# Two interleaved mixers on one TensorE queue: its order taken from the source, value products one key block later, PSUM banks rearranged

## The chip, the cores and the metric

One NeuronCore of a Trainium2 chip runs the whole kernel. The metric is the device time of one execution in microseconds (us). An engine runs its own queue of instructions in order: PE is TensorE (matmuls), DVE VectorE, ACT ScalarE, POOL GpSimd, SP the queue that issues most transfers.

## What is computed

The reference is an encoder block of one layer (2048 tokens, width 1024). Its first half mixes tokens: one projection feeds a bidirectional softmax attention (8 heads of 64, two key heads) and a bidirectional RWKV-7 recurrence (8 heads of 64); their outputs are joined, projected and added. Its second half is an expert-choice mixture of 16 SwiGLU experts. The part that the change touches:

```python
s = jnp.einsum('bqhgd,bkhd->bhgqk', qi, k, preferred_element_type=jnp.float32) * scale
p = jax.nn.softmax(s, axis=-1).astype(v.dtype)
o = jnp.einsum('bhgqk,bkhd->bqhgd', p, v)
...
sa = jnp.einsum('bhvk,bhk->bhv', S, -kk_t)
S = (S * w_t[:, :, None, :] + sa[..., None] * (kk_t * a_t)[:, :, None, :]
     + v_t[..., None] * k_t[:, :, None, :])
y_t = jnp.einsum('bhvk,bhk->bhv', S, r_t)
```

## The kernel before, in words

The program has four parts: `phase1` (projections and preparation, to about 720 us), `mixers` (attention and recurrence together, to about 2375 us), `out_proj` and `moe`. Only `mixers` changes. It draws on two Python generators in turn, `rwkv` and `attention`, which record instructions. A scheduler then sets the order on each engine from priorities and its own times, so PE's order is not the source's.

**Attention** has 16 blocks of 512 queries (for two heads). A block walks over 16 key blocks `kb`. For each: four matmuls make the scores (tile `st`, one buffer of two banks, L707 and L708), ACT takes the exponential into a tile `pt` (L709, four buffers, `PTB`), DVE and POOL add `pt` to the row sums `acc` (L712). After four key blocks a group of eight matmuls multiplies the four `pt` with the values (tile `o_ps`, L694), at high priority and before the scores of the next key block; it begins with the `pt` that came last. At a block's end `sum_ps` (L674), a reciprocal of 512 columns (L676) and a product finish it. Meanwhile `att_max` finds the maxima for the next block: 32 pairs of matmuls into `s_ps` (L648, L649, two banks) and 32 DVE reductions (L650). Block 7 is the last of the first key head; there the next block's maxima wait for new keys.

**Recurrence**: 16 groups `n` (four pairs of heads, two directions, two halves of the sequence), each of four quarters `k`, each quarter of four turns `j` (one `yield` a turn). A quarter `i` does: `rq_step` (L1030, the state of the quarter before, ACT scales it at L1035) in every turn; `rq_l` (tile `l_ps`, L1013, into `lc` by ACT L1015 and DVE L1016) in turns 0 and 1; `a1_rows` (four transposes, L852) in turn 2; `rq_av` (two transposes of `al` into `av_ps`, L980) and `rq_wu` (L1001) in turn 3. Two jobs are put off (`self.tiled`) until the next value group, and `flush` records them behind it: `a1_products` (L865, into the banks of `st`; two DVE products with a mask take it out, L870) and the products into `av_ps` (L988; ACT copies all of it into `r4`, L990). `rq_wu` multiplies `r4` with the group's inverse `tt`.

Three banks serve this: `pa` (transposes, merge), `pb` (`av_ps`, `wu_ps`, both halves of `l_ps`), `pc` (steps). One tile holds a bank until the last reader is done.

The inverse `tt` of group `n+1` is made during group `n`: `rw_solve` (30 elimination steps of two small operations, L901 and L903, for nine groups all on DVE, for seven all on POOL; three steps a turn in quarters 0 to 2), a round of transfers through DRAM, and `rw_merge` in quarter 3: transfers into `bdn`, `bdr`, `tt`; eight matmuls `z_ps` (L940, ACT copy L941), eight `x_ps` (L946), four ACT copies into `tt` (L949).

Of the kernel before, what the change touches and what calls it, by code (L numbers as in the profile page):

```python
# [12 lines left out]
ALU = mybir.AluOpType  # L13
# [570 lines left out]
PTB = 4  # L584
# [5 lines left out]
class Attention(Encoder):  # L590
# [32 lines left out]
    def att_max(self, j, qc, keys, res):  # L623
# [5 lines left out]
        for h in range(2):  # L629
            qd = self.a_q.tile([P, 512], F32, tag="q_raw", name="q_raw")  # L630
# [31 lines left out]
        mt = self.a_q.tile([16, P], F32, tag="mt", name="mt")  # L662
# [7 lines left out]
    def att_finish(self, j, qc, av, acc):  # L670
# [9 lines left out]
    def att_out(self, keys, v, q):  # L680
        nc = self.nc
        khh, kl1 = keys
        qs, q2 = q
        av = self.o_ps.tile([P, 512], F32, tag="o", name="o_ps")
        acc = self.a_l.tile([P, 2, 512], F32, tag="acc", name="acc")
        pts = {}

        def group(k0):
            with self.tc.high_priority():

                for kb in (k0 + 3, k0, k0 + 1, k0 + 2):
                    pt = pts.pop(kb)
                    for h in range(2):
                        last = nc.tensor.matmul(av[64 * h : 64 * h + 64, :], v[:, kb, :], pt[:, h, :], start=(kb == 3), stop=(kb == 14), tile_position=(0, 64 * h))  # L694
                with self.tc.issue_after(last.ins):
                    self.behind = self.flush() or last.ins

        for kb in range(16):
            ks = slice(kb * P, (kb + 1) * P)

            if kb % 4 == 0 and kb:
                group(kb - 4)
            pt = self.a_p.tile([P, 2, 512], F32, tag="pt", name="pt", bufs=PTB)
            pts[kb] = pt
            s = self.o_ps.tile([P, 2, 512], F32, tag="st", name="st_ps", bufs=1)
            for h in range(2):
                nc.tensor.matmul(s[:, h, :], khh[:, ks], qs[h], start=True, stop=False)  # L707
                nc.tensor.matmul(s[:, h, :], kl1[:, ks], q2[h], start=False, stop=True)  # L708
            nc.scalar.activation(out=pt, in_=s, func=AF.Exp, scale=0.125)  # L709
            if kb:  # L710
                for h, eng in enumerate((nc.gpsimd if kb % 8 == 3 else nc.vector, nc.gpsimd)):
                    eng.tensor_tensor(out=acc[:, h, :], in0=(first if kb == 1 else acc)[:, h, :], in1=pt[:, h, :], op=ALU.add)  # L712
            else:
                first = pt
            if kb >= 6 and self.block in MOD_BLOCKS:
                next(self.rest, None)
            yield
        group(12)
        self.att_done = av, acc

    def attention(self):

# [6 lines left out]
        while more:  # L729
# [3 lines left out]
            if n % 3 == 0:  # L733
                yield
        v = self.att_values(0)
        done = None
        for n, (j, qc) in enumerate(blocks):
            if n == 7:
                nxt, nq, late = None, [], True
            else:  # L740
                nq, late = [], False
                nxt = self.att_max(*blocks[n + 1], keys, nq) if n + 1 < 16 else iter(())
            if done:
                self.att_finish(*done)
            self.block = n
            for _ in self.att_out(keys, v, cur):
                if not late:
                    for _ in range(3):
                        next(nxt, None)
                yield  # L750
            done = (j, qc) + self.att_done
            if late:
                keys = self.att_keys(1)
                for i, _ in enumerate(self.att_max(*blocks[n + 1], keys, nq)):
                    if i % 3 == 2:
                        yield
# [5 lines left out]
        self.att_finish(*done)  # L762
# [8 lines left out]
SOLVE_DVE = (0, 2, 4, 5, 7, 8, 11, 12, 14)  # L771


class Rwkv(Attention):
# [110 lines left out]
    def rw_solve(self, n, g):  # L885
# [3 lines left out]
        eng = nc.vector if n in SOLVE_DVE else nc.gpsimd  # L889
# [82 lines left out]
    def rq_av(self, Q):  # L972
# [5 lines left out]
        p3 = self.bank("pb").tile([P, 2, 4, 64], F32, tag="p", name="av_ps")  # L978
        for i in range(2):
            nc.tensor.transpose(p3[:, i, 0:4:3, :], Q["al"][:, i, :], self.ident)  # L980
        lv = l56.rearrange("p c (x k) -> p c x k", k=64)

        def products():
            for r in range(2):
                for h in range(2):
                    for par in range(2):
                        c = 2 * r + par
                        last = nc.tensor.matmul(p3[64 * par : 64 * par + 64, r, 1 + h, :], r56[64:128, c, 192 * h : 192 * h + 64],  # L988
# [670 lines left out]
```

## Time and profile before

| | us |
|---|---|
| median of 3 runs (3774.88 to 3779.12) | 3778.05 |
| the profiled execution | 3788.53 |
| its span in the trace | 3786.8 |
| PE busy in the span | 3415.4 (90%) |
| DVE, ACT, POOL busy | 2529.6, 1737.5, 1513.7 |

Busy time of PE is the time in which at least one matmul is in flight; a slow clock makes it longer. PEclk is the clock granted to TensorE as a share of full speed.

### The profile page before, as it was taken

The numbers are of one execution on the slowest core, as the hardware profiler recorded it, in microseconds if no ns is written. First come the engines' busy times: TensorE is split into PE (matmuls) and PEld (weight loads), VectorE is DVE, ScalarE is ACT, GpSimd is POOL, SyncE is SP. The second block draws the span as 40 slices with busy tenths as digits, with TensorE's granted clock in tenths as the row PEclk, the third lists the DMA queues.
The fourth block names the chain that finished last, engine by engine and source line by source line (L and its number), as shares of the span: only waits on it lengthen the run. The fifth ranks groups of instructions, "written<-read, shape, count | busy, mean of one in ns | idle before, by whom it ended". The sixth has DMA issues, their size and how long they took to land. (4 is left out here: it accounts for less than half of the span.)

```text
span 3786.8 us, 61015 instructions
## 1 busy us (share of the span) xinstructions
PE 3415.4 (90%) x23196; PEld 2811.8 (74%) x23196; DVE 2529.6 (67%) x4289; ACT 1737.5 (46%) x3050; POOL 1513.7 (40%) x1484
## 2 busy tenths in 40 slices
PE   6998899779988888898889998994999999999998
PEld 5887888656666566576666665773899999999997
DVE  5788788875858957665886866446565665655653
ACT  4445444415554455445555565222344444444443
POOL 3444345516363363456347275332332322322321
PEclk8999999779998999889999998997999999999999
DMA  5335333443323433433333322443566766766764
GB/s 180 106 126 174 105 117 137 145 129 74 86 66 89 105 90 73 101 81 87 86 83 92 79 69 80 155 151 117 165 214 212 215 215 205 223 201 217 222 200 129
DMA packets 531866, 511.16 MB, mean 135 GB/s; under 512 B 213624, under 2 KB 450530, under 8 KB 526452
## 3 DMA queue, kind: packets, MB, share of 16 engines
q1 hardware_dynamic: 521252, 472.34, 40.6%
q0 software_dynamic: 10000, 34.91, 4.0%
q8 instruction: 183, 3.00, 0.3%
q14 instruction: 111, 0.91, 0.1%
q10 hardware_dynamic: 320, 0.00, 0.0%
HBM read 392.70 MB, written 109.20 MB: 133 GB/s over the span
## 5 line engine op out<-in xcount | busy, mean ns | idle before, releaser
L1496 DVE TENSOR_TENSOR w_lo<-w_raw,w_hi 128x2048 fp32r<-128x2048 f32 x189 | 432.8, 2295 | 385.9 <-ACT w_hi L1493 385.3
L1560 PE MATMUL gu<-hh,w_lo 128*128 128x256 f32 x2048 | 573.3, 280 | 0.0
L1560 PE MATMUL gu<-hl,w_hi 128*128 128x256 f32 x2048 | 572.4, 280 | 0.0
L1560 PE MATMUL gu<-hh,w_hi 128*128 128x256 f32 x2048 | 572.4, 280 | 0.0
L712 POOL TENSOR_TENSOR acc<-acc,pt 128x512 f32<-128x512 f32 x256 | 346.6, 1359 | 507.2 <-ACT pt L709 471.0
L1493 ACT CAST w_hi<-w_raw 128x2048 fp32r<-128x2048 f32 x192 | 366.9, 1912 | 320.0 <-PE down L1583 133.3
L650 DVE TENSOR_REDUCE mx<-s_ps 128x1 f32<-128x512 f32 x512 | 337.6, 681 | 131.1 <-PE s_ps L649 128.6
L247 PE MATMUL proj_ps<-hh,w_hi 128*128 128x258 f32 (+1 forms) x1280 | 375.4, 294 | 32.9 <-DVE s_k L265 23.9
L1560 PEld LDWEIGHTS gu<-hh,w_lo 128*128 128x128 f32 x2048 | 387.8, 189 | 0.0
L1560 PEld LDWEIGHTS gu<-hh,w_hi 128*128 128x128 f32 x2048 | 385.5, 188 | 1.3
L1560 PEld LDWEIGHTS gu<-hl,w_hi 128*128 128x128 f32 x2048 | 385.5, 188 | 1.4
L247 PE MATMUL proj_ps<-hl,w_hi 128*128 128x258 f32 (+1 forms) x1280 | 373.1, 292 | 6.4 <-DVE hl L149 5.9
L247 PE MATMUL proj_ps<-hh,w_lo 128*128 128x258 f32 (+1 forms) x1280 | 371.6, 290 | 0.0
L709 ACT ACTIVATE pt<-st_ps 128x1024 f32<-128x1024 f32 x256 | 262.1, 1024 | 209.1 <-PE st_ps L708 168.5
L149 POOL TENSOR_TENSOR dl<-hid,dh 128x256 fp32r<-128x256 f32 x128 | 135.1, 1055 | 448.1 <-ACT dh L148 447.8
L694 PE MATMUL o_ps<-pt,av 128*64 128x512 f32 x1024 | 269.9, 675 | 27.5 <-ACT pt L709 27.2
L247 PEld LDWEIGHTS proj_ps<-hh,w_hi 128*128 128x128 f32 x1280 | 250.9, 196 | 41.8 <-issue 23.0
L648 PE MATMUL s_ps<-khh,qhl 128*128 128x512 f32 x512 | 239.7, 469 | 33.5 <-DVE mx L650 28.4
L707 PE MATMUL st_ps<-qhl,khh 128*128 128x512 f32 x512 | 231.8, 453 | 38.0 <-DVE r L870 31.5
L247 PEld LDWEIGHTS proj_ps<-hl,w_hi 128*128 128x128 f32 x1280 | 251.5, 197 | 10.6 <-DVE hl L149 6.6
L247 PEld LDWEIGHTS proj_ps<-hh,w_lo 128*128 128x128 f32 x1280 | 250.7, 196 | 2.1 <-issue 1.1
L712 DVE TENSOR_TENSOR acc<-acc,pt 128x512 f32<-128x512 f32 x192 | 189.0, 984 | 63.4 <-ACT pt L709 60.4
(418 smaller groups left out, 7979.2 us busy)
## 6 DMA issues: line engine op xcount, KB each, us to landing
w_raw<-in_w_gate_dram SPq DMA_DIRECT2D x64, 1024.0 KB
w_raw<-in_w_up_e_dram SPq DMA_DIRECT2D x64, 1024.0 KB
w_raw<-in_w_down_dram SPq DMA_DIRECT2D x64, 1024.0 KB
d_x<-X SPq DMA_DIRECT2D x32, 1024.0 KB
xin<-d_x SPq DMA_DIRECT2D x64, 512.0 KB
w_raw<-in_w_in_dram SPq DMA_DIRECT2D x80, 256.0 KB
mod_w<-in_w_ada_dram SPq DMA_DIRECT2D x64, 256.0 KB
mod_w<-in_w_ada_dram SPq DMA_DIRECT2D x8, 1024.0 KB
```

The lines of the kernel that those rows point to most:

```text
L149: (eng or nc.gpsimd).tensor_tensor(out=lo, in0=src, in1=hi.bitcast(F32), op=ALU.subtract)
L247: nc.tensor.matmul(acc[:, :n], a[:, kt, :], b[:, kt, lo : lo + n], start=(kt == 0 and m == 0), stop=(kt == KT - 1 and m == 2))
L648: nc.tensor.matmul(s, qs[h][:, ts], khh[:, ks], start=True, stop=False)
L650: nc.vector.tensor_reduce(out=mx[:, 4 * h + qt, kc : kc + 1], in_=s, axis=AX.X, op=ALU.max)
L694: last = nc.tensor.matmul(av[64 * h : 64 * h + 64, :], v[:, kb, :], pt[:, h, :], start=(kb == 3), stop=(kb == 14), tile_position=(0, 64 * h))
L707: nc.tensor.matmul(s[:, h, :], khh[:, ks], qs[h], start=True, stop=False)
L709: nc.scalar.activation(out=pt, in_=s, func=AF.Exp, scale=0.125)
L712: eng.tensor_tensor(out=acc[:, h, :], in0=(first if kb == 1 else acc)[:, h, :], in1=pt[:, h, :], op=ALU.add)
L1493: nc.scalar.copy(out=hi, in_=raw)
L1496: eng.tensor_tensor(out=lo, in0=raw, in1=hi.bitcast(F32), op=ALU.subtract)
L1560: nc.tensor.matmul(acc[:, m, :], a[:, kt, i * P : (i + 1) * P], b[:, kt, :], start=(kt == 0 and n == 0), stop=(kt == KT - 1 and n == 2))
```

## The change

PE's order inside `mixers` is now the source's (`manual_schedule`); the other engines are still ordered by the scheduler. The two generators are drawn on in small parts: `yield False` ends a part, `yield True` a turn, and the two alternate part by part until both have ended the turn. A value group is recorded after the scores of the next key block (for a block's last group after the first scores of the next block), with the sums' matmuls behind it; `pt` gets a fifth buffer, two small tiles lose their second. The transposes of `al` go to bank `pa` with their own ACT copy, the second half of `l_ps` to `pa` too. Every solve has its first 12 steps on DVE and the other 18 on POOL. In quarter 3 the merge's transfers are issued in turn 0, `z_ps` in turn 2, `x_ps` in turn 3. The reciprocal is four of 128 columns. A gap in `out_proj`'s memory map grows by 1536 bytes.

```diff
@@ constants @@
-PTB = 4
+PTB = 5
...
-SOLVE_DVE = (0, 2, 4, 5, 7, 8, 11, 12, 14)
+SOLVE_DVE = 12
@@ att_finish: the sums' matmuls leave it, the reciprocal in four pieces @@
-        sm = self.a_ps.tile([P, 512], F32, tag="s", name="sum_ps", bufs=SB)
-        for h in range(2):
-            nc.tensor.matmul(sm[64 * h : 64 * h + 64, :], self.ones[:, 0:64], acc[:, h, :], start=True, stop=True, tile_position=(0, 64 * h))
         rec = self.a_l.tile([P, 512], F32, tag="rec", name="rec")
-        nc.vector.reciprocal(out=rec, in_=sm)
+        for c in range(0, 512, P):
+            nc.vector.reciprocal(out=rec[:, c : c + P], in_=sm[:, c : c + P])
@@ att_out becomes att_values_of, att_scores, att_sums @@
-            with self.tc.high_priority():
-
-                for kb in (k0 + 3, k0, k0 + 1, k0 + 2):
...
+    def att_values_of(self, B, k0):
...
+        with self.tc.issue_after(B["st"]):
+            for kb in range(k0, k0 + 4):
+                pt = B["pts"].pop(kb)
+                for h in range(2):
+                    last = nc.tensor.matmul(av[64 * h : 64 * h + 64, :], v[:, kb, :], pt[:, h, :], start=(kb == 0), stop=(kb == 15), tile_position=(0, 64 * h))
+            if k0 == 12:
+                sm = self.a_ps.tile([P, 512], F32, tag="s", name="sum_ps", bufs=SB)
...
+        with self.tc.issue_after(last.ins):
+            self.behind = self.flush() or last.ins
+        if k0 == 12:
+            self.att_finish(*B["id"], av, sm)
@@ attention: one key block a turn, in small steps @@
+            for kb in range(16):
+                for i in range(4 if kb % 4 == 2 else 3):
+                    if kb % 4 or kb == i:
+                        next(nxt, None)
+                    yield False
+                self.att_scores(B, kb)
+                if kb % 4 == 0 and (kb or last):
+                    if kb == 0:
+                        last["st"] = B["st"]
+                    self.att_values_of(B if kb else last, kb - 4 if kb else 12)
+                if kb:
+                    self.att_sums(B, kb)
...
+                yield True
@@ rw_solve @@
-        eng = nc.vector if n in SOLVE_DVE else nc.gpsimd
...
         for i in range(1, 31):
...
+            eng = nc.vector if i <= SOLVE_DVE else nc.gpsimd
@@ rq_av @@
-        p3 = self.bank("pb").tile([P, 2, 4, 64], F32, tag="p", name="av_ps")
+        pt = self.bank("pa").tile([P, 2, 2, 64], F32, tag="p", name="al_ps")
         for i in range(2):
-            nc.tensor.transpose(p3[:, i, 0:4:3, :], Q["al"][:, i, :], self.ident)
+            nc.tensor.transpose(pt[:, i], Q["al"][:, i, :], self.ident)
+        r4v = r4.rearrange("p r (x k) -> p r x k", k=64)
+        nc.scalar.copy(out=r4v[:, :, 0:4:3, :], in_=pt)
...
         def products():
+            p3 = self.bank("pb").tile([P, 2, 2, 64], F32, tag="p", name="av_ps")
...
-            nc.scalar.copy(out=r4, in_=p3.rearrange("p r x k -> p r (x k)"))
+            nc.scalar.copy(out=r4v[:, :, 1:3, :], in_=p3)
@@ rq_l @@
-        p5 = self.bank("pb").tile([P, 4, P], F32, tag="p", name="l_ps")
+        p5 = self.bank("pa" if h else "pb").tile([P, 4, P], F32, tag="p", name="l_ps")
@@ rwkv: extra(j), and each turn j in three parts @@
-                if k == j == 0:
-                    pass
-                elif k < 3:
-                    run(solve, 3)
-                else:
+                if k < 3:
+                    run(solve, 3 if k + j else 0)
+                elif j == 0:
                     run(solve)
+                    run(merge, 1)
+                elif j == 2:
                     run(merge, 2)
                 run(fin, 1)
...
             step(0)
+            yield False
             self.rq_l(Qs[i], 0)
...
+            yield False
             extra(0)
-            yield
+            yield True
@@ mixers @@
-        streams = [self.rwkv(), self.attention()]
-        n = 0
-        while streams:
-            n += 1
-            for g in list(streams):
-                if len(streams) == 2 and g is streams[1] and n % 4 == 0 and n <= 12:
-                    continue
-                if next(g, "end") == "end":
-                    streams.remove(g)
+        streams = [self.attention(), self.rwkv()]
+        with self.tc.manual_schedule(engines={mybir.EngineType.PE}):
+            n = 0
+            while streams:
+                n += 1
+
+                turn = [g for g in streams if len(streams) == 1 or g is streams[1] or n % 4 or n > 12]
+                while turn:
+                    for g in list(turn):
+                        done = next(g, "end")
+                        if done:
+                            turn.remove(g)
+                        if done == "end":
+                            streams.remove(g)
```

On PE, at the end of a quarter, the value group with what hangs on it stands like this before (`o_ps` values, `av_ps` and `p` the two put-off jobs, `s_ps_` with a number the recurrence's step, `s_ps` the maxima, `st_ps` scores):

```order
L694 MATMUL o_ps<-pt,av 64x512 x8
L988 MATMUL av_ps<-l_0_8385,r_10367 64x64 x8
L865 MATMUL p_11756<-xin 128x128 x8
L1030 MATMUL s_ps_11790<-sr_8373,lc 128x64 x2
L648 MATMUL s_ps<-khh,qhl 128x512
L649 MATMUL s_ps<-kl_8312,qa 128x512
L648 MATMUL s_ps<-khh,qhl 128x512
L649 MATMUL s_ps<-kl_8312,qa 128x512
L1001 MATMUL wu_ps<-r_11519,tt_8368 128x128 x4
L1030 MATMUL s_ps_11790<-sr_8374,lc 128x64 x2
L707 MATMUL st_ps<-qhl,khh 128x512
```

and at the same place in the change:

```order
L988 MATMUL al_ps<-ident,al 128x128 x2
L1012 MATMUL wu_ps<-r_11538,tt_8368 128x128 x4
L710 MATMUL st_ps<-qhl,khh 128x512
L711 MATMUL st_ps<-qa,kl_8312 128x512
L710 MATMUL st_ps<-qhl,khh 128x512
L711 MATMUL st_ps<-qa,kl_8312 128x512
L689 MATMUL o_ps<-pt,av 64x512 x8
L999 MATMUL av_ps<-l_0_8385,r_10388 64x64 x8
L873 MATMUL p_11792<-xin 128x128 x8
L648 MATMUL s_ps<-khh,qhl 128x512
L649 MATMUL s_ps<-kl_8312,qa 128x512
L1041 MATMUL s_ps_11811<-sr_8373,lc 128x64 x2
```

`wu` and the next scores have moved ahead of the value group.

In the merge's quarter, PE has this before:

```order
L946 MATMUL x_ps<-rb,z 128x32 x8
L648 MATMUL s_ps<-khh,qhl 128x512
L649 MATMUL s_ps<-kl_8312,qa 128x512
L694 MATMUL o_ps<-pt,av 64x512 x8
L988 MATMUL av_ps<-l_1_8386,r_10190 64x64 x8
L865 MATMUL p_11547<-xin 128x128 x8
L1030 MATMUL s_ps_11581<-sr_8375,lc 128x64 x2
```

and in the change:

```order
L860 MATMUL p_11489<-ident,xin 128x128 x4
L648 MATMUL s_ps<-khh,qhl 128x512
L649 MATMUL s_ps<-kl_8312,qa 128x512
L948 MATMUL z_ps<-bdr,bdn 128x128 x8
L710 MATMUL st_ps<-qhl,khh 128x512
L711 MATMUL st_ps<-qa,kl_8312 128x512
L710 MATMUL st_ps<-qhl,khh 128x512
L711 MATMUL st_ps<-qa,kl_8312 128x512
L1041 MATMUL s_ps_11392<-sr_8374,lc 128x64 x2
L988 MATMUL al_ps<-ident,al 128x128 x2
L954 MATMUL x_ps<-rb,z 128x32 x8
L1012 MATMUL wu_ps<-r_11318,tt_8368 128x128 x4
```

`wu`, which reads what ACT makes of `x_ps`, now stands right behind it; the eight `z_ps` stand together.

## Rows read from the trace of the kernel before

**Rows 1.** The page's slices of the span: PE busy and granted clock, in tenths.
```profile
PE   6998899779988888898889998994999999999998
...
PEclk8999999779998999889999998997999999999999
```

**Rows 2.** Busy time by stretch: us, then busy us (instructions) of PE, PEld, DVE, ACT, POOL, PEclk, DMA.
```profile
720.00:865.00 145.00, 101.26 (x481) 67.45 (x481) 113.09 (x207) 34.47 (x57) 52.49 (x53) 0.73 0.49 133
865.00:2280.00 1415.00, 1263.56 (x7923) 897.60 (x7923) 996.95 (x1615) 746.81 (x1514) 689.37 (x780) 0.93 0.34 84
...
1328.00:1376.00 48.00, 47.11 (x317) 35.65 (x316) 29.55 (x43) 26.61 (x56) 36.87 (x53) 1.00 0.29 72
```

**Rows 3.** What PE waited for, 865 to 2280 us: total us, times, longest us.
```profile
PE o_ps L694 <- ACT pt L709: 25.7, 17, 2.2
PE st_ps L707 <- DVE r L870: 23.1, 15, 5.6
PE z_ps L940 <- DMA bdr<-d_rt: 22.2, 9, 6.0
PE s_ps L648 <- DVE mx L650: 16.9, 27, 2.6
PE av_ps L980 <- DVE lc L1016: 16.6, 19, 1.7
PE l_ps L1013 <- DVE lc L1016: 15.2, 15, 3.0
```

**Rows 4.** Timeline of ACT: start, us; one L990 copy a quarter; a merge's copies.
```profile
929.63 0.59 ACT L990 COPY r<-av_ps 128x512 f32<-128x512 f32 x1 [3.27 <-PE av_ps L988]
...
1391.72 0.59 ACT L990 COPY r<-av_ps 128x512 f32<-128x512 f32 x1 [4.28 <-PE av_ps L988]
...
1408.56 0.59 ACT L941 COPY z<-z_ps 128x512 f32<-128x512 f32 x1 [0.15 <-PE z_ps L940]
1416.22 1.50 ACT L949 COPY tt<-x_ps 32x256 f32<-32x256 f32 x4 [0.55 <-PE x_ps L946]
1424.98 0.59 ACT L990 COPY r<-av_ps 128x512 f32<-128x512 f32 x1 [5.61 <-PE av_ps L988]
...
2040.69 0.59 ACT L990 COPY r<-av_ps 128x512 f32<-128x512 f32 x1 [2.56 <-PE av_ps L988]
2060.81 0.59 ACT L990 COPY r<-av_ps 128x512 f32<-128x512 f32 x1 [4.37 <-PE av_ps L988]
...
2286.01 0.59 ACT L990 COPY r<-av_ps 128x512 f32<-128x512 f32 x1 [0.19 <-PE av_ps L988]
```

**Rows 5.** Timeline of PE in a merge's quarter: start, us, [idle before <-releaser].
```profile
1395.95 1.05 PE L1001 MATMUL wu_ps<-r,tt 128*128 128x128 f32 x8
1402.23 2.05 PE L940 MATMUL z_ps<-bdr,bdn 128*128 128x128 f32 x8 [5.23 <-DMA bdr<-d_rt]
...
1404.79 0.77 PE L707 MATMUL st_ps<-qhl,khh 128*128 128x512 f32 x1
...
1407.46 1.06 PE L940 MATMUL z_ps<-bdr,bdn 128*128 128x128 f32 x8
```

**Rows 6.** Groups by shape, 865 to 2280 us: busy us, mean ns | idle before.
```profile
L709 ACT ACTIVATE pt<-st_ps 128x1024 f32<-128x1024 f32 x230 | 235.5, 1024 | 149.7 <-PE st_ps L708 110.5 <-issue 25.6 <-POOL ts L903 6.4
...
L870 DVE TENSOR_TENSOR r<-p,mask 128x512 f32<-128x512 f32 x112 | 72.0, 683 | 135.3 <-PE p L865 134.8 <-PE l_ps L1013 0.5
L676 DVE RECIPROCAL rec<-sum_ps 128x512 f32<-128x512 f32 x14 | 47.0, 3356 | 11.3 <-PE sum_ps L674 11.3
...
L712 POOL TENSOR_TENSOR acc<-acc,pt 128x512 f32<-128x512 f32 x230 | 309.7, 1351 | 457.6 <-ACT pt L709 421.6 <-ACT mt L663 10.5 <-DVE gn_m L63 9.9
...
L903 POOL TENSOR_TENSOR ts<-ts,ts_t 64x240 f32<-64x240 f32 x14 | 10.3, 734 | 0.6
L901 POOL TENSOR_TENSOR ts_t<-ts 64x234 f32<-64x234 f32 x14 | 9.3, 665 | 0.9
```

**Rows 7.** Timeline of PE at the start of the mixers: start, us, [idle before <-releaser].
```profile
736.68 1.20 PE L648 MATMUL s_ps<-khh,qhl 128*128 128x512 f32 x2
...
763.99 1.16 PE L865 MATMUL p<-xin 64*128 64x128 f32 x16 [0.62 <-ACT vt L339]
...
846.75 1.13 PE L940 MATMUL z_ps<-bdr,bdn 128*128 128x128 f32 x8 [0.56 <-DMA bdr<-d_rt]
```

More of the change, by code (lines that the diff above doesn't have):

```diff
@@ L677, in att_finish @@
         nc.vector.tensor_tensor(out=rec, in0=av, in1=rec, op=ALU.mult)
         (nc.gpsimd if (j, qc) == (3, 3) else nc.sync).dma_start(out=self.d_o[j, :, qc * 512 : (qc + 1) * 512], in_=rec)
-    def att_out(self, keys, v, q):
+    def att_values_of(self, B, k0):
         nc = self.nc
[L682 to L688, printed above, removed]
-            with self.tc.high_priority():
-                for kb in (k0 + 3, k0, k0 + 1, k0 + 2):
[L692 to L712, printed above, removed]
-            else:
-                first = pt
-            if kb >= 6 and self.block in MOD_BLOCKS:
-                next(self.rest, None)
-            yield
-        group(12)
-        self.att_done = av, acc
@@ new lines, in att_values_of @@
+        if k0 == 0:
+            B["av"] = self.o_ps.tile([P, 512], F32, tag="o", name="o_ps")
+        av, v = B["av"], B["v"]
+        with self.tc.issue_after(B["st"]):
[5 more added lines that the diff above has]
+                sm = self.a_ps.tile([P, 512], F32, tag="s", name="sum_ps", bufs=SB)
+                for h in range(2):
+                    last = nc.tensor.matmul(sm[64 * h : 64 * h + 64, :], self.ones[:, 0:64], B["acc"][:, h, :], start=True, stop=True, tile_position=(0, 64 * h))
@@ new lines, in att_values_of, with att_scores @@
+        with self.tc.issue_after(last.ins):
+            self.behind = self.flush() or last.ins
+        if k0 == 12:
+            self.att_finish(*B["id"], av, sm)
+    def att_scores(self, B, kb):
+        nc = self.nc
+        khh, kl1 = B["keys"]
+        qs, q2 = B["q"]
+        ks = slice(kb * P, (kb + 1) * P)
+        if kb == 0:
+            B["acc"] = self.a_l.tile([P, 2, 512], F32, tag="acc", name="acc")
+        pt = B["pts"][kb] = self.a_p.tile([P, 2, 512], F32, tag="pt", name="pt", bufs=PTB)
+        s = self.o_ps.tile([P, 2, 512], F32, tag="st", name="st_ps", bufs=1)
+        for h in range(2):
+            nc.tensor.matmul(s[:, h, :], khh[:, ks], qs[h], start=True, stop=False)
+            B["st"] = nc.tensor.matmul(s[:, h, :], kl1[:, ks], q2[h], start=False, stop=True).ins
+        nc.scalar.activation(out=pt, in_=s, func=AF.Exp, scale=0.125)
@@ L721, in attention, with att_sums @@
+    def att_sums(self, B, kb):
+        nc = self.nc
+        acc, pt = B["acc"], B["pts"][kb]
+        for h, eng in enumerate((nc.gpsimd if kb % 8 == 3 else nc.vector, nc.gpsimd)):
+            eng.tensor_tensor(out=acc[:, h, :], in0=(B["pts"][0] if kb == 1 else acc)[:, h, :], in1=pt[:, h, :], op=ALU.add)
     def attention(self):
@@ L733, in attention @@
             if n % 3 == 0:
-                yield
+                yield True
         v = self.att_values(0)
[L736 to L748, printed above, removed]
-                        next(nxt, None)
-                yield
-            done = (j, qc) + self.att_done
+        last = None
+        for n, id_ in enumerate(blocks):
+            late = n == 7
+            nq = []
+            nxt = iter(()) if late or n == 15 else self.att_max(*blocks[n + 1], keys, nq)
+            B = dict(id=id_, keys=keys, q=cur, v=v, pts={})
+            for kb in range(16):
+                for i in range(4 if kb % 4 == 2 else 3):
+                    if kb % 4 or kb == i:
+                        next(nxt, None)
+                    yield False
+                self.att_scores(B, kb)
+                if kb % 4 == 0 and (kb or last):
+                    if kb == 0:
+                        last["st"] = B["st"]
+                    self.att_values_of(B if kb else last, kb - 4 if kb else 12)
+                if kb:
+                    self.att_sums(B, kb)
+                if kb >= 6 and n in MOD_BLOCKS:
+                    next(self.rest, None)
+                yield True
+            last = B
             if late:
+                self.att_values_of(B, 12)
+                last = None
                 keys = self.att_keys(1)
                 for i, _ in enumerate(self.att_max(*blocks[n + 1], keys, nq)):
-                    if i % 3 == 2:
-                        yield
+                    yield i % 3 == 2
                 v = self.att_values(1)
@@ L761, in attention @@
             cur = nq
-        self.att_finish(*done)
+        self.att_values_of(B, 12)
 from functools import partial
@@ L1190, in rwkv @@
             self.rq_step(last, j)
-            yield
+            yield True
         for _ in chain(fin, self.rq_done(last, *quarters[-1])):
-            yield
+            yield True
     def rq_done(self, Q, n, k):
```

28 lines of the change are left out of this document (16 added, 12 removed).

## The prediction

> **What bounds the kernel now.** I read four views, in this order. First the slices of the page: outside the mixers PE is close to full, while from 720 to 2375 us, slices 8 to 25, it shows 8 and 9 and a granted clock between 7 and 9 [rows 1]. Only this stretch changes, so only it is costed. Second, busy time by stretch: in the 1415 us from 865 to 2280, PE is busy 1263.6 and idle 151.4; DVE is busy 997, ACT 747, POOL 689 [rows 2]. No other engine is near full, so PE with its waits sets the pace. The granted clock is 0.93 on average. Between its two levels of 1.2 and 2.4 GHz that is 14% of the time at the lower. At full clock the stretch 1328 to 1376 spends 47.11 us on 317 instructions, 0.149 us each [rows 2]. By that the 7923 of the long stretch would cost about 1177 us, so some 86 us of its busy time is slow clock (an estimate: the mix of instructions differs somewhat). Idle and slow clock belong together. Behind an idle time of 5.23 us eight `z_ps` take 2.05 us, and a little later eight more take 1.06 [rows 5].
>
> Third, who ended PE's idle time [rows 3]: six waits make 119.7 of the 151.4 us. Fourth, one ACT copy per quarter gives the quarters' lengths: the best is 20.1 us (2040.69 to 2060.81), one with a merge 33.3 (1391.72 to 1424.98), and from 929.63 to 2286.01 there are 56 quarters, 24.2 us each [rows 4].
>
> **The change, part by part.** Waits that go:
>
> - *Values behind the next scores: 25.7 us.* The group now stands behind scores which themselves wait for the last exponential (1.02 us [rows 6]), so its inputs are there. That exponential is covered by the step, the two `al` transposes and `wu`, 14 instructions at 0.149 us [rows 2], about 2.1 us. I cost the scores' own wait at nothing. If ACT takes other copies first, some tenths of a microsecond come back per quarter. The fifth `pt` buffer is what the later group needs.
> - *Scores behind the mask products: 23.1 us.* `a1_products` fills the banks of the scores, and DVE needs twice 0.68 us to empty them [rows 6]. Before, the next scores can come soon behind it. Now the next ones are those of the following turn, with three pairs of maxima, a step and half of `l_ps` ahead, 18 instructions, some 2.7 us.
> - *Banks: 16.6 + 15.2 us.* `al` and both halves of `l_ps` waited in one bank for DVE's `lc`. They now alternate, each with most of a turn in between. `wu` no longer has to stand behind the flush either, since `al` does not hold its bank. This shortens the chain by which a quarter hands over to the next, but has no idle time of its own in the list.
> - *Merge's transfers: 22.2 us.* Two turns, some 11 us, now lie between their issue and `z_ps`. The longest wait was 6.0.
>
> Together 102.8 us. Two things I leave at zero. Maxima still have two banks, so their 16.9 us stays. Each reciprocal of 3.36 us [rows 6] becomes four pieces with the same sum, between which DVE can serve a maximum.
>
> Costs that come:
>
> - *`wu` right behind `x_ps`.* It waits for ACT's four copies, 1.50 us [rows 4]. The bounds are 0 (were they done in time) and 2.5 (an exponential of 1.02 goes first); I take the copies alone. 15 groups by 1.5 is 22 us.
> - *`z_ps` in one piece.* The second four need the bank, so the copy of 0.59 us [rows 4] stands between: 15 by 0.6 is 9. Bounds 0 and 15 us.
> - *The start.* Before, 15 pairs of maxima run between 736.68 and 763.99 while PE waits for phase 1's last part; now only two stand there. The first `z_ps` is at 846.75 [rows 7], set by the first solve, so the recurrence starts as before. But attention then has less behind it: 13 pairs at DVE's pace of one every 0.7 us, about 9 us. I take 10, with bounds 0 and 30, the time in which PE could stand idle before that `z_ps`.
> - *Solve split.* DVE loses work and POOL gains some, neither on PE's path if in time: nothing here, a rival below.
>
> Net idle: 102.8 less 31 is 72, almost half of 151.4. I let the slow clock's 86 us shrink in the same proportion, by 41. Idle time in the other half remains, and with it slow stretches. Sum: -72 - 41 + 10 = -103. The profiled execution took 3788.5 us, 1.7 more than its span and 0.28% more than the median. So 3685 for a profiled execution, and by the same step **3675 for the median**. Between them the bounds of the unknown costs move this by -31 (both new waits nothing) to +41 (both and the start at their upper ends), the clock's share by some 40 either way.
>
> **A rule that speaks against it.** In the trace PE holds still for 5.23 us at `z_ps`, with the next scores issued 2.6 us behind it [rows 5]: what stands behind a waiting matmul waits too. The Trainium skill, "TensorE: Matmul & The Clock Gate", section "Step-by-step: what each phase is for", says that only weight loads are pulled ahead and matmuls stay in program order; the trace agrees. By that rule alone an order fixed in the source could only lose where its guess of readiness is worse than the scheduler's, which is the last rival.
>
> **The rivals.**
>
> *Nearly everything goes (0.13).* If the shorter hand-over also takes the 48.6 us of idle time that I leave, and with it the other 45 of slow clock, another 94 us go: about 3580. For it: quarters of 20.1 us exist, and 64 quarters at 20.9 (that, and a share of the merge) would save even more, 64 by 3.3. Against: those quarters hold no merge, and DVE at 997 of 1415 us cannot always be on time.
>
> *The waits only move (0.12).* DVE still reduces 32 maxima a block at 0.68 us, and with PE's order fixed each pair waits for a bank in turn. If the wait for maxima takes 60 us that before were hidden, 40 to 45 are left of the gain: about 3735, and with somewhat more no difference can be told. A measurement of this kernel tells about 0.2%, 7.6 us, from no change. For it: that wait is already there 27 times [rows 3]. Against: DVE loses more than a third of the solve's work that it had.
>
> *Slower, because POOL comes late (0.13).* From turn 1 of quarter 1 to turn 3 of quarter 2 POOL has 18 steps of up to 0.67 + 0.73 us and about eight adds of 1.35 [rows 6]: up to 25 + 11 = 36 us in seven turns, 42 us at today's pace and 39 at the forecast's. If POOL falls behind, adds hold the `pt` buffers and the solve ends late. From one turn (5.6 us) too late, the transfers no longer arrive before `z_ps`, and PE waits with all of attention behind it. Two turns, 11 us, in each of 15 groups make 165 us. Against the gain of 103 that is 62 slower: about 3840. For it: the margin is small, and before the scheduler could fill such a wait. Against: seven groups were solved on POOL alone before, all 30 steps, and the two turns of slack are new.
>
> That the order would not be the source's can be left out: the built order shows it.
>
> **How the numbers follow.** Forecast 0.62, rivals 0.13, 0.12 and 0.13. Faster by over 0.2%: the forecast, the first rival and half of the second, 0.81. Within 0.2%: the other half, 0.06. Slower: 0.13. The range reaches from 3585, near the first rival, to 3800, which takes in the second and the light forms of the third; it leaves out some 0.17.
>
> **What would show it.** In the profile of the changed kernel the waits of `o_ps` for `pt`, of `st_ps` for the mask product and of `av_ps` and `l_ps` for `lc` should be under 5 us each from the first step to the last, and `z_ps` should hardly wait for a transfer. `wu_ps` should appear with some 20 us behind the copies into `tt`. The granted clock of the mixers should be 0.95 or more, and a quarter 22 to 22.5 us. It is wrong if `s_ps` behind `mx`, or `st_ps` behind `pt`, rises above 60 us, or if `z_ps` waits for transfers in most groups.

## The result, and the profile after

The changed kernel takes 3968.24 us (median of 4 runs, 3965.77 to 3972.35), beside it the kernel before 3778.59. The ratio is 1.0505, 95% interval 1.0487 to 1.0523: **190 us slower**, where 3675 us and a gain of 103 were forecast. Range and sign are both missed.

The page of the changed kernel: span, busy times, and the slices with PE's busy share and granted clock.

```profile
span 3966.7 us, 61206 instructions
...
PE 3482.3 (88%) x23196; PEld 2893.4 (73%) x23196; DVE 2457.8 (62%) x4163; ACT 1756.9 (44%) x3114; POOL 1637.7 (41%) x1658
...
PE   7997998588888888878887888999499999999998
...
PEclk9998999679897888878888989999699999999999
```

The span grew by 179.9 us. PE runs 23196 matmuls in both kernels. Its idle time (span less busy) rose from 371.4 to 484.4 us, by 113.0; its busy time for the same matmuls rose by 66.9. In the slices of [rows 1] the mixers showed 8 and 9 with some 7; now 8 is the rule, and the clock shows 8 where it showed 9.

Busy time by stretch, and below it the two quarters that stand one behind the other at about 1008 to 1068 us (columns as in [rows 2]). The second is the merge's.

```profile
720.00:865.00 145.00, 83.60 (x357) 54.30 (x357) 98.94 (x171) 27.80 (x47) 58.42 (x67) 0.62 0.44 120
865.00:2470.00 1605.00, 1354.01 (x8084) 995.70 (x8081) 930.99 (x1521) 773.50 (x1588) 804.41 (x939) 0.87 0.30 75
...
1007.97:1027.82 19.85, 17.85 (x121) 11.90 (x123) 7.89 (x13) 14.93 (x31) 18.19 (x32) 1.00 0.26 68
1027.82:1067.95 40.13, 31.36 (x164) 23.64 (x166) 20.98 (x30) 13.90 (x31) 10.96 (x7) 0.79 0.39 102
```

A plain quarter reaches 19.85 us at full clock. That is no gain on the best of before: the 20.1 us of [rows 4] is not the shortest quarter there; the one from 2217.47 to 2236.11 takes 18.64, with PE busy for 18.54. A merge quarter takes 40.13, of which PE is idle for 8.8, at a clock of 0.79. Measured like this from one copy out of `av_ps` to the next, the 15 merge quarters take 35.7 us on average, and 26.4 in the kernel before; the first quarters of the groups changed from 21.4 to 20.8.

What PE waited for, 865 to 2470 us (total us, times, longest):

```profile
PE s_ps L648 <- DVE mx L650: 69.2, 51, 5.2
PE x_ps L954 <- ACT r L990: 37.5, 15, 3.0
PE m_ps L661 <- DVE mhl L657: 23.6, 14, 3.6
PE z_ps L948 <- DMA bdr<-d_rt: 20.2, 5, 9.8
PE st_ps L710 <- DVE r L878: 19.0, 8, 4.2
PE al_ps L988 <- DVE gl_in L1109: 13.8, 5, 5.0
PE wu_ps L1012 <- ACT tt L957: 12.4, 15, 0.8
PE s_ps L648 <- DVE rec L675: 12.0, 13, 1.9
PE z_ps L948 <- ACT z L949: 10.7, 15, 0.7
PE yT_ps L1103 <- DVE lc L1027: 10.5, 6, 2.7
```

Of the six waits of [rows 3], that of `o_ps` for `pt` and those of `av_ps` and `l_ps` for `lc` are gone. The scores' wait for the mask product and the merge's for its transfer have hardly moved. The maxima's has grown fourfold, and seven of these rows have no counterpart there (of `m_ps` the trace of before has 4.0 us). One of them is a wait that moved: `yT_ps` takes the bank `pa`, in which the second half of `l_ps` now waits for DVE's `lc`.

The matmuls of that merge quarter on PE (start, us, [idle before <-releaser]):

```profile
1040.57 0.80 PE L648 MATMUL s_ps<-khh,qhl 128*128 128x512 f32 x1 [3.70 <-DVE mx L650]
...
1047.59 1.16 PE L948 MATMUL z_ps<-bdr,bdn 128*128 128x128 f32 x8
...
1049.46 1.16 PE L948 MATMUL z_ps<-bdr,bdn 128*128 128x128 f32 x8 [0.72 <-ACT z L949]
...
1051.79 0.39 PE L988 MATMUL al_ps<-ident,al 128*128 128x128 f32 x2
...
1054.84 3.62 PE L954 MATMUL x_ps<-rb,z 128*128 128x32 f32 x16 [2.66 <-ACT r L990]
...
1059.29 2.08 PE L1012 MATMUL wu_ps<-r,tt 128*128 128x128 f32 x8 [0.82 <-ACT tt L957]
```

What DVE did ahead of the first of these waits, and ACT ahead of the third:

```profile
1039.43 0.49 DVE L1235 TENSOR_SCALAR mod_acc<-mod_w,cond 128x512 f32<-128x512 f32 x1 [3.47 <-DMA d_o<-rec]
1039.83 0.68 DVE L650 TENSOR_REDUCE mx<-s_ps 128x1 f32<-128x512 f32 x1
```

```profile
1051.60 1.02 ACT L712 ACTIVATE pt<-st_ps 128x1024 f32<-128x1024 f32 x1 [0.35 <-PE st_ps L711]
1052.65 0.64 ACT L1046 ACTIVATE sr<-s_ps,pc 64x64 f32<-64x64 f32 x2
1053.32 1.07 ACT L1054 COPY y<-s_ps 64x128 f32<-64x128 f32 x4
1054.42 0.37 ACT L990 COPY r<-al_ps 128x256 f32<-128x256 f32 x1
```

A maximum that could have run stands in DVE's queue behind the first product of another sum (L1235) that waits 3.47 us for an output transfer to free its tile, and all of PE's queue stands behind the next `s_ps`. Then `x_ps` wants the bank `pa` that the `al` transposes have just taken, and the copy that frees it is fourth in ACT's queue. The next eight `wu_ps` take 2.08 us, at a granted clock of 0.50 (the lower of its two levels) from 1054.8 to 1061.3; in the plain quarter before, at 1.00, eight took 1.06. That the queues of ScalarE and VectorE hold to their order is also what the Trainium skill, "PSUM — Partial Sum Buffer", section "Engine vs sequencer instructions", states (strict first in, first out); the two rows on DVE agree.

### The profile page after: what moved, and what is told of

Its sections match the earlier page's. It is cut to its first block, busy times and chain, and to the rows that moved or that the text cites. A ratio compares the mean times of both kernels' runs of the same rounds, so it can differ in the third digit from the quotient of the medians.

```text
span 3966.7 us, 61206 instructions
## 1 busy us (share of the span) xinstructions
PE 3482.3 (88%) x23196; PEld 2893.4 (73%) x23196; DVE 2457.8 (62%) x4163; ACT 1756.9 (44%) x3114; POOL 1637.7 (41%) x1658
## 5 line engine op out<-in xcount | busy, mean ns | idle before, releaser
L718 POOL TENSOR_TENSOR acc<-acc,pt 128x512 f32<-128x512 f32 x256 | 370.0, 1450 | 619.6 <-ACT pt L712 601.7
L648 PE MATMUL s_ps<-khh,qhl 128*128 128x512 f32 x512 | 264.1, 516 | 99.4 <-DVE mx L650 82.7
L247 PEld LDWEIGHTS proj_ps<-hh,w_hi 128*128 128x128 f32 x1280 | 250.4, 196 | 42.3 <-issue 23.8
L710 PE MATMUL st_ps<-qhl,khh 128*128 128x512 f32 x512 | 243.8, 476 | 40.2 <-DVE r L878 23.4
L689 PE MATMUL o_ps<-pt,av 128*64 128x512 f32 x1024 | 245.5, 623 | 0.0
```

The costliest lines, as they stand in the source:

```text
L247: nc.tensor.matmul(acc[:, :n], a[:, kt, :], b[:, kt, lo : lo + n], start=(kt == 0 and m == 0), stop=(kt == KT - 1 and m == 2))
L648: nc.tensor.matmul(s, qs[h][:, ts], khh[:, ks], start=True, stop=False)
L718: eng.tensor_tensor(out=acc[:, h, :], in0=(B["pts"][0] if kb == 1 else acc)[:, h, :], in1=pt[:, h, :], op=ALU.add)
```

## The experiments

Each has three rounds or five beside the kernel before, whose median lay between 3779 and 3783 us in the batches. Two theories carry most expectations: **A**, PE held to the source's order stands still at inputs that come late, above all in the merge quarter; **B**, the late inputs are DVE's doing, whose queue is still in the scheduler's order. Beside them stand **C**, the split solve makes POOL and DVE late, and **D**, the banks or the later value products cost by themselves.

### The order alone

```diff
-        with self.tc.manual_schedule(engines={mybir.EngineType.PE}):
+        with ExitStack():
```

> The change with one thing undone: PE's order inside the mixers is the scheduler's again; the small turns, the later value groups, the banks, the split solve and the spread merge stay. Theory A (PE, held to the source's order, stands still at matmuls whose inputs are late, above all in the merge's quarter, and its clock falls): the time comes back to 3700 to 3800 us, a merge's quarter to under 29 us. Theory B (DVE's queue, which the scheduler orders by its own times, holds ready maxima behind row-sum adds that wait): about half comes back, 3850 to 3900. Theory C (the split solve makes POOL and DVE late) and theory D (banks or later values cost by themselves): it stays over 3900.

Measured: 3771.66 us, ratio 0.9972 (0.9959 to 0.9986). So the fixed order costs 197 us with the rest of the change in place, and that rest, in the scheduler's order, is worth 8. The time is theory A's. From the sixth copy out of `av_ps` to the last, a quarter takes 23.2 us here and 26.3 in the change; a merge quarter by itself can't be compared, since the scheduler moves the copies by which it is measured. The waits of PE in 865 to 2470 us:

```profile
PE st_ps L710 <- ACT pt L712: 33.3, 36, 4.0
PE s_ps L648 <- DVE mx L650: 21.9, 28, 2.2
...
PE z_ps L948 <- DMA bdr<-d_rt: 11.2, 3, 4.7
```

Same code, same banks: the maxima cost 21.9 instead of 69.2 us, and `x_ps` waits 0.3 us instead of 37.5. One thing more differs: the scheduler orders DVE anew when PE's order is its own. DVE waits 300.6 us for `pt` at the row sums in the change and 126.9 here. How much of the 197 us is DVE's order was not separated.

### The merge quarter's order

`x_ps` ahead of the `al` transposes, `wu_ps` behind the value group.

```diff
+            if k == 3:
+                run(merge)
             if i + 2 < len(quarters):
                 self.rq_av(Qs[i + 2])
...
                 if k == 3:
-                    run(merge)
+                    yield False
+                    yield False
                 self.rq_wu(Qs[i + 1])
```

> The change with the merge's quarter written in another order: x_ps stands ahead of the al transposes, and wu of that quarter behind the value group. Theory A: the waits of x_ps for the al copy (37.5 us) and of wu for the copies into tt (12.4 us) go, the granted clock of a merge's quarter rises from about 0.8 to 0.9 or more, and the quarter falls from 35.7 to about 30 us: 3860 to 3900 in all. Theory B: these waits go, but PE stops at the next maxima instead: 3920 to 3950. Theory C or D: 3920 or more.

Measured: 3952.93 us, ratio 1.0458 (1.044 to 1.0475), 15 us back of the 197. Theory A's 3860 to 3900 us is missed: a merge quarter falls to 32.6 us where 30 was expected. The waits of `x_ps` and `wu_ps` are gone, but their bank hands them on:

```profile
PE s_ps L648 <- DVE mx L650: 71.1, 51, 5.7
PE al_ps L988 <- ACT tt L957: 32.9, 15, 2.6
```

### The split of the solve

```diff
-SOLVE_DVE = 12
+SOLVE_DVE = (0, 2, 4, 5, 7, 8, 11, 12, 14)
...
-            eng = nc.vector if i <= SOLVE_DVE else nc.gpsimd
+            eng = nc.vector if n in SOLVE_DVE else nc.gpsimd
```

> The change with the solves as before: nine groups wholly on DVE, seven wholly on POOL. Theory C: at least 50 us come back, 3915 or less. Theories A, B and D: 3955 to 3985, DVE busier and POOL less busy by some tens of us.

Measured: 3973.84 us, ratio 1.0514 (1.0497 to 1.0532). That is what all but theory C expected: the split is not the cause, and the prediction's third rival falls.

### DVE in the source's order too

```diff
-        with self.tc.manual_schedule(engines={mybir.EngineType.PE}):
+        with self.tc.manual_schedule(engines={mybir.EngineType.PE, mybir.EngineType.DVE}):
```

> The change with DVE too in the order of the source. Theory B: DVE's wait for pt falls from 300 us to under 100, PE's wait for mx from 69 to under 30, the time to 3870 to 3920. Theory A: the merge's quarter keeps its waits, 3940 to 3980. If DVE stands still at the source's solve steps and merges instead, it is slower than 3980.

Measured: 4092.66 us, ratio 1.0814 (1.079 to 1.0838), 124 us worse still. PE's waits for the maxima rise to 83.6 us. DVE's wait for `pt` does fall, from 300.6 to 124.0 us, but at the mask products it now waits 434.9 us for `p` (78.6 in the change). A second queue held to the source doesn't heal the first. Whether a better order of DVE would is not shown by this.

### The merge quarter's banks

The second experiment and, beside it:

```diff
-            pz = self.bank("pa").tile([P, 4, P], F32, tag="p", name="z_ps")
+            pz = self.bank("pa" if q else "pb").tile([P, 4, P], F32, tag="p", name="z_ps")
...
-        px = self.bank("pa").tile([P, 8, 32], F32, tag="p", name="x_ps")
+        px = self.bank("pb").tile([P, 8, 32], F32, tag="p", name="x_ps")
```

> The second experiment's merge quarter (x_ps ahead of the transposes of al, wu_ps behind the value group), and beside it x_ps and the first half of z in the bank pb instead of pa, so that x_ps, al_ps, z_ps and the products of the quarter no longer stand behind each other's copies in one bank. Theory A (TensorE, held to the source's order, stands still at inputs that come late, in the merge quarters above all): al_ps behind the tt copies falls from 32.9 us to under 10, the merge quarter from 32.6 us to under 30, and with 15 of them the time comes to 3900 to 3935 us. Theory B (VectorE's queue is what makes the inputs late): 3940 to 3960 us, the waits only move to z_ps and s_ps. Theory D (banks and later value products cost by themselves): slower than the second experiment's 3953 us.

Measured: 3852.64 us, ratio 1.0175 (1.0152 to 1.0197): 100 us from two bank names. Theory A's mechanism holds: `al_ps` behind the copies into `tt` is gone from the list, and the gain is almost twice the most that it gave (18 to 53 us). In the merge quarter looked at above, `z_ps`, `x_ps` and what follows now stand without a wait, at full clock from 1041.5 us on:

```profile
1041.51 1.95 PE L948 MATMUL z_ps<-bdr,bdn 128*128 128x128 f32 x16
...
1044.62 1.92 PE L954 MATMUL x_ps<-rb,z 128*128 128x32 f32 x16
...
1046.38 0.41 PE L988 MATMUL al_ps<-ident,al 128*128 128x128 f32 x2
...
1047.66 3.65 PE L689 MATMUL o_ps<-pt,av 128*64 128x512 f32 x16
1051.25 0.68 PE L999 MATMUL av_ps<-l,r 64*64 64x64 f32 x16
1051.86 1.16 PE L873 MATMUL p<-xin 64*128 64x128 f32 x16
```

A merge quarter takes 25.9 us on average (32.6 in the second experiment). Against that experiment, idle time fell by 55.4 us (483.2 to 427.8) and busy time by 42.8 (3467.7 to 3424.9), at a mean granted clock of 0.927 instead of 0.916: a good part came back as clock.

### Priorities on DVE, and a transpose that moves the streams

Sixth, on the change: the maxima and (written the same way) the mask products at high priority, the transpose of the maxima (`m_ps`) two turns later. Seventh: the same on the fifth.

```diff
+                    with self.tc.high_priority():
-                    nc.vector.tensor_reduce(out=mx[:, 4 * h + qt, kc : kc + 1], in_=s, axis=AX.X, op=ALU.max)
+                        nc.vector.tensor_reduce(out=mx[:, 4 * h + qt, kc : kc + 1], in_=s, axis=AX.X, op=ALU.max)
...
         yield
+        yield
+        yield
 
         pm = self.a_ps.tile([P, 512], F32, tag="s", name="m_ps", bufs=SB)
```

> The changed kernel with the block maxima and the mask products at high priority on VectorE, and the transpose of the maxima two small turns later; TensorE's order is otherwise the same. Theory B: s_ps behind mx falls from 69.2 us to under 25, st_ps behind r from 19.0 to under 8, m_ps from 23.6 to under 8, and the time by some 80 us, to 3870 to 3910 us. Theory A without B: what goes at these rows comes back at the copies of al and tt and at the transfers; 3940 to 3975 us.

> The fifth and sixth experiments together. If the loss of 190 us is nothing but head-of-line waits of TensorE at the named inputs (theories A and B together), the two gains add: 3800 to 3870 us, with a granted clock of 0.90 or more between 865 and 2470 us. If the waits are taken over by the next late input each time (an order that was written without regard to when the inputs come loses wherever it stands), the gain is under half of the sum and the time stays above 3880 us.

Measured: 4072.34 us (1.0755, 1.0732 to 1.0778) and 3993.04 us (1.0548, 1.0521 to 1.0574): both over 100 us *slower* than without the edits, which no theory had. The ninth takes the two `yield` lines alone, on the fifth:

> The fifth experiment (mended merge quarter, 3853 us) with one edit more: the transpose of the maxima stands two small turns later in TensorE's order, so that VectorE has time for the small work before it. Theory A (each late input in the fixed order costs its wait): m_ps behind mhl falls from 23.0 us to under 5, and the time by 15 to 25 us, to 3828 to 3838 us. If a wait that goes only moves to the next late input: 3845 to 3860 us, with s_ps, st_ps or al_ps longer by as much.

Measured: 3995.25 us (1.0574, 1.0558 to 1.0589), like the seventh: so the priorities do nothing measurable, and the two lines cost 142 us. Their first effect isn't the transpose. The first block's maxima are prepared ahead by the same generator, some calls a turn; there the two calls more end in one turn more, and the whole attention stream runs one key block later against the recurrence. The products `av_ps` and `p` then stand three blocks behind a value group instead of right behind it. Two runs separate slip and edit.

```diff
-                turn = [g for g in streams if len(streams) == 1 or g is streams[1] or n % 4 or n > 12]
+                turn = [g for g in streams if len(streams) == 1 or g is streams[1] or n % 4 or n > 16]
```

> The fifth experiment (3853 us) with nothing changed but the start of the attention stream, one block later against the recurrence: the deferred products av_ps and p of the recurrence then stand three blocks of scores behind a value group instead of right behind it. If the slip is what made the sixth, seventh and ninth experiments slow: 3970 to 4010 us, with av_ps behind the copy of l over 30 us and p behind pt over 20 us, as in the ninth. If it was the transpose of the maxima itself: 3840 to 3870 us.

Measured (the slip alone): 3980.48 us, ratio 1.0517 (1.0487 to 1.0548), 128 us more than the fifth. The place of the slipped products on PE, and PE's waits in 865 to 2470 us:

```profile
1021.14 1.06 PE L1012 MATMUL wu_ps<-r,tt 128*128 128x128 f32 x8
...
1025.02 0.68 PE L999 MATMUL av_ps<-l,r 64*64 64x64 f32 x16 [1.90 <-ACT l L1014]
...
1027.35 2.08 PE L873 MATMUL p<-xin 64*128 64x128 f32 x16 [1.65 <-ACT pt L712]
...
1033.49 3.65 PE L689 MATMUL o_ps<-pt,av 128*64 128x512 f32 x16
```

```profile
PE av_ps L999 <- ACT l L1014: 50.7, 50, 2.3
PE s_ps L648 <- DVE rec L675: 30.7, 12, 2.6
PE p L873 <- ACT pt L712: 29.5, 36, 2.0
```

`av_ps` shares the bank `pb` with `wu_ps`, `p` the banks of the scores. In the right place the value group's 3.65 us stand between and cover ACT's copy and exponential; in the slipped place one block of scores does, some 1 us.

> The ninth experiment's edit (the transpose of the maxima two small turns later, on the fifth experiment) with the attention stream started one block earlier, so that the deferred products stand right behind the value groups again. If the slip was the cause in the ninth (3995 us): m_ps behind mhl under 5 us, and 3825 to 3850 us, below the fifth by up to the 23 us of that wait. If the edit itself is the cause: over 3950 us.

Measured (the two `yield` lines, and `n > 8` in the line above): 3817.33 us, ratio 1.0093 (1.0066 to 1.0121), 35 us below the fifth. `m_ps` waits 6.7 us instead of 23.0. The two lines thus cost 142 us, or go with a gain of 35, by where the streams stand to each other. The gain is more than that one wait; the maxima wait 9 us less too. The earlier start alone, without the two lines, was not run.

### The banks in the kernel before

In the kernel before, `rq_av` as in the change (its part of the diff above) and:

```diff
-        p5 = self.bank("pb").tile([P, 4, P], F32, tag="p", name="l_ps")
+        p5 = self.bank("pa" if h else "pb").tile([P, 4, P], F32, tag="p", name="l_ps")
```

> The kernel before (order from the scheduler) with the bank rearrangement alone: the transposes of al in a tile of their own in pa with a copy of their own, and the second half of l_ps in pa. Theory A: the banks are worth nothing or a few us while the scheduler moves work past a late copy: 3765 to 3785 us, the waits of av_ps and l_ps behind lc (31.8 us in the kernel before) shorter. Theory D: slower than the kernel before by over 10 us, 3790 us or more.

Measured: 3792.25 us, ratio 1.0015 (0.9999 to 1.003). No gain, and no loss that can be told (the interval allows one of up to 11 us). Yet the waits of `av_ps` and `l_ps` for `lc` are gone from the list of 865 to 2280 us. Others took their place, maxima (16.9 us before) and scores (2.6) above all:

```profile
PE s_ps L648 <- DVE mx L650: 32.6, 34, 2.4
...
PE st_ps L707 <- ACT pt L709: 20.5, 22, 1.9
```

PE's idle time in the span is 375.0 us, and 371.4 in the kernel before. So even under the scheduler a wait that is taken off the list need not be won.

### Relief for DVE, and everything under one order or the other

Tenth, on the fifth:

```diff
-SOLVE_DVE = 12
+SOLVE_DVE = 4
```

> The fifth experiment with the steps 5 to 12 of each triangular solve on GpSimd instead of VectorE, which takes some 100 us of work from VectorE in 865 to 2470 us (12 steps take 152 us there) and the bursts that stand ahead of the maxima. Theory B (VectorE's queue makes the maxima late): s_ps behind mx falls from 72 us to under 45, and the time to 3800 to 3835 us. Against it: the solve comes later on GpSimd (0.6 us a step where VectorE takes 0.4), z_ps behind its transfer rises from 15.8 us to over 40, and the time stays at 3845 us or more.

Measured: 3810.98 us, ratio 1.0082 (1.0067 to 1.0096), 42 us below the fifth: theory B's time, with both mechanisms at once:

```profile
PE s_ps L648 <- DVE mx L650: 48.0, 53, 3.8
PE z_ps L948 <- DMA bdr<-d_rt: 41.5, 10, 10.7
...
PE st_ps L710 <- DVE r L878: 7.0, 7, 2.0
```

The maxima's wait falls by 24 us and the scores' wait for the mask product from 17.8 to 7.0 (theory B has a part), while the later solve costs 26 at the transfers.

Fifteenth: this edit and the fourteenth's together.

> All that was found under the fixed order together: the mended merge quarter and its banks, eight of the solve's steps on GpSimd (tenth experiment, 3811 us), and the transpose of the maxima two turns later with the streams' place kept. If the waits add: 3785 to 3805 us, about the kernel before. If the wait of m_ps only moves: 3805 to 3820 us.

Measured: 3825.21 us, ratio 1.0117 (1.0083 to 1.0151). The two gains don't add; the time is above both ranges. Under the fixed order nothing tried reaches the kernel before.

Eleventh: the fifth with the first experiment's edit, so in the scheduler's order.

> The fifth experiment's kernel (mended merge quarter and its banks) with the scheduler's order instead of the source's. Theory A (what the fixed order loses is waits at late inputs, which the scheduler moves other work past): the mended merge quarter is worth little here, 3755 to 3780 us, and the fixed order alone still costs 70 to 100 us beside it (3853). If the merge quarter's banks were a cost under any order: under 3750 us.

Measured: **3754.35 us, ratio 0.9931 (0.9917 to 0.9945)**, the fastest version here, faster than before and than the first experiment. Mending the merge quarter is worth 17 us there, and 116 under the fixed order.

Twelfth, on the first experiment:

```diff
+                    with self.tc.high_priority():
-                    self.att_values_of(B if kb else last, kb - 4 if kb else 12)
+                        self.att_values_of(B if kb else last, kb - 4 if kb else 12)
```

> The first experiment (everything of the change but the fixed order, 3772 us) with the value products at high priority for the scheduler, as in the kernel before. If the waits of st_ps behind pt (33.3 us in the first experiment, 6.0 before) come from value products that stand too late: they fall under 10 us and the time to 3745 to 3765 us. If the scheduler's order needs no help: 3765 to 3780 us.

Measured: 3767.97 us, ratio 0.9972 (0.996 to 0.9985), as the first experiment. But the wait of `st_ps` for `pt` fell only to 24.9 us, not under 10, so what that wait is worth to the scheduler's order stays open; the priority gains nothing.

Sixteenth: the eleventh with `SOLVE_DVE = 4`.

> The eleventh experiment (scheduler's order, mended merge quarter and banks, 3754 us) with eight of the solve's steps on GpSimd, as in the tenth. If VectorE's queue limits the scheduler's order too: 3720 to 3745 us. If the scheduler moves other work past a late maximum anyway: 3745 to 3770 us.

Measured: 3771.7 us, ratio 0.9975 (0.9957 to 0.9992), 17 us above the eleventh, so neither side had it. The maxima's wait falls (29.1 to 22.2 us) and the merge's for its transfer rises (5.2 to 19.2). Where the scheduler can go round a late maximum, the later solve costs more than the relief of DVE gains.

## Why the prediction was wrong

- **The step that failed is the sum's frame: it took the list of waits of before as the list of waits that a fixed order can have.** It subtracted what the edits remove from [rows 3] and left what is not in it, or small in it, at zero ("Maxima still have two banks, so their 16.9 us stays"). But that list, made under the scheduler, holds only what the scheduler could not go round. The first experiment shows it: the same code with the scheduler's order has 21.9 us at the maxima, with the fixed order 69.2, and the fixed order costs 197 us. The prediction's own sign of being wrong, over 60 us at the maxima, came. Taking waits off the list is no gain by itself either: with the banks alone, in the kernel before, the 31.8 us went and the time did not. The prediction quoted the rule that decides ("an order fixed in the source could only lose where its guess of readiness is worse than the scheduler's") and gave it 0.13, through POOL alone.
- *Waits that go.* `o_ps` 25.7 and `av_ps` with `l_ps` 31.8 went, as said. The scores' 23.1 became 19.0: 2.7 us of cover are too short when the mask product stands behind other work in DVE's queue, in six of the eight cases solve steps. The merge's 22.2 became 20.2: two turns suffice in ten groups and fail by up to 9.8 us in five. Of 102.8 us some 64 went, and 10.5 of these came back for `lc` at `yT_ps`.
- *Costs named.* The halves of `z_ps` cost 10.7 us (9 taken), `wu` behind `x_ps` 12.4, half of the 22 taken. In the first 145 us PE is busy 17.7 us less than in [rows 2] (10 taken, bound 30).
- *Costs not named.* Maxima +52; `x_ps` behind the `al` copy 37.5; `m_ps` +20; `al_ps` behind DVE's `gl_in` 13.8; the maxima's banks behind the reciprocal 12.0; `yT_ps` 10.5. Together some 146 us. With the 23 named and the 64 that went this makes 105, and PE's idle time grew by 99.6 (151.4 in the 1415 us of [rows 2], 251.0 in the 1605 above). The change's diff showed the second: `al_ps` and `x_ps` in `pa`, one right behind the other in the order printed above. The text costed `wu_ps` there and passed over the instruction ahead of it.
- *The clock.* It was to follow idle time down, by 41 us; busy time followed idle time up, by 66.9, and the mean granted clock of the span fell from 0.940 to 0.914.
- *The rivals.* The second named the maxima and 60 us, rightly, but as one wait beside a gain that stands. The third had the right sign from the wrong place: the solve's split changes nothing, and with more of it on POOL the kernel was faster. Its prices, and the first rival's, stand on two misread lengths: from 929.63 to 2286.01 there are 57 quarters of 23.8 us, not 56 of 24.2, and 20.1 us is not the best. Neither is in the sum.
- *What was left out:* where two streams stand to each other. In the change it was the better of the two tried, but it was worth 128 us, and nothing in the prediction depended on it.

Of the 190 us, the merge quarter's order and banks account for 116 and the later transpose, with the streams' place kept, for 35; the remaining 39 to the kernel before, and 63 to the eleventh experiment, were not taken apart further; maxima, transfers and `al` inputs are the longest rows left, and DVE's own order may have a part. How much of it a different fixed order could recover was not tried.

## What to carry to other kernels

The waits of a scheduled kernel are those its scheduler could not hide, so before an in-order queue is given a fixed order, ask of each instruction which engine frees its bank or makes its input, and what stands ahead of that in the other engine's queue. Run the rest of the change without the fixed order first: here the order was the whole loss, and the rest 8 us of gain. With two streams on one queue, their place to each other is a parameter like any other: put what waits for a copy right behind the longest work that waits for nothing, and look at that place again after every edit that adds a turn.

## What the runs showed that was not expected

Busy time for the same 23196 matmuls does not follow idle time in proportion, as the prediction assumed, and a difference in it need not be clock. The tenth experiment has 406.5 us of idle time (3809.3 less 3402.8) and 3402.8 busy, at a mean granted clock of 0.934; the first has 336.2 idle (3780.8 less 3444.6) and 3444.6 busy, at 0.939. So the first is busy for 42 us more at a clock that is no lower. The traces show a reason. The two matmuls of the sums, one for each head, write the two halves of one tile (`sum_ps`, 64 columns each). In the tenth experiment they stand together:

```profile
918.64 1.03 PE L693 MATMUL sum_ps<-acc,ones 128*64 128x512 f32 x4
```

In the first, the scheduler put a pair of maxima between them:

```profile
920.61 1.02 PE L693 MATMUL sum_ps<-acc,ones 128*64 128x512 f32 x2
...
922.22 1.07 PE L693 MATMUL sum_ps<-acc,ones 128*64 128x512 f32 x2
```

Side by side, four instructions take as long as two alone. Over the whole kernel the 64 instructions of `sum_ps` keep PE busy for 22.2 us in the tenth experiment and 31.5 in the first, at nearly the same length each (599 and 605 ns). The value groups, written for two halves as well, are also broken up more often in the first. An estimate: with each moment of busy time weighed by the granted clock in the trace, PE has 3241 us of work at full clock in the tenth experiment and 3280 in the first, so all but some 3 of the 42 us are not clock. Weighed like this the kernel before has 3255 us and the changed one 3237: the source's order packs the matmuls closer by 18 us, and the clock costs some 85 of busy time, more than the 66.9 that the page shows.

Where the clock was low is seen in the rows above: the slow 2.08 and 3.62 us matmul runs come right behind several waits within one quarter, and the plain quarter ahead of them, with 2.0 us idle, ran at full clock. What length or spacing of idle time decides was not separated.
